# Sums of squares, decay sums and row broadcasts of a hybrid decoder trunk, put on TensorE in another form

## The chip, the cores and the metric

The kernel runs on one core of one Trainium2 chip, as one program in one launch. The metric is device time in microseconds (us); the engines are TensorE (PE, with its weight loads PEld), VectorE (DVE), ScalarE (ACT), GpSimd (POOL) and SyncE's DMA queue (SP).

## The reference

Two layers work on 512 tokens of width 1024. Each has a token-mixing part and a SwiGLU channel part of hidden width 2816, each behind an RMS norm with scale and shift from a conditioning vector. The mixing part projects the normed input once and feeds three causal mixers, whose outputs (512 + 256 + 256 columns) go through one output projection.

- A is a gated DeltaNet with four heads of width 128. Its queries and keys are normed per head, `x * rsqrt(sum(x*x) + 1e-6)`. With the gates g (16 numbers for each position of a 128-token block: 4 blocks and 4 heads) it needs the decay between any two positions, `exp(gcum[i] - gcum[j])` for i >= j, where gcum is the running sum of g.
- B is a chunked spatial-gating MLP.
- C is a sliding-window softmax attention with three patterns of window and dilation. The patterns' outputs are merged with weights that come from the softmax denominators: one number per token and head, times the 64 outputs of that head.

## The kernel before

Activations lie transposed: 128 channels in the partitions, 512 tokens along the free axis, so that a projection streams 512 columns. Exact float32 products are made of three one-pass matmuls: every weight tile and every activation tile is split into a rounded part `hi` (type fp32r, written by ScalarE) and the rest `lo` (VectorE), and `mm3` adds hi*hi, hi*lo and lo*hi. Small products stay in float32, which TensorE does in several passes; the trace shows them as two instructions.

The program is a set of tasks (Python generators). A planner (`Plan`, `Engine`) keeps a model of when each engine will be free, with costs per instruction, and at each step lets the task of best priority write its next instructions. The order of instructions on each engine is the order in which they were written; the engines work their queues in order. Priorities of the tasks stand in `PR0` and `PR1`, one set for each layer. Work tiles of 128x512 (`slot`) come from an arena of 58, PSUM banks (`bank`) from eight.

What the change touches:

- `loader` issues the weights' DMAs through four raw buffers; a transfer waits until the buffer four places before it is free. In the opening, each of eight chunks of the input needs two modulation reductions on VectorE, a scale on ScalarE, a product on VectorE, a rounded part on ScalarE and a low part on VectorE, and one weight tile; then 24 one-pass matmuls of the first projection use it. With the last of these weight tiles the loader also issues the DMA of the constant matrices (`cst`, among them the triangles `triu` and `slow`).
- `inv_rms` gives the norms' row scales: sums over channels by matmuls with one moving column, a reciprocal root on VectorE, and then a matmul for each block of 128 tokens that broadcasts the scales over the partitions. It is called for all four blocks in the opening and for half the tokens at a time in the six half norms after it.
- `sumsq_heads` gives the sums of squares of queries or keys. It is called for the keys (`kss`) and for the queries (`qss`) in both layers. ScalarE squares a head; a matmul with 32 columns of ones writes the sums to 32 partitions of one bank; after four heads ScalarE copies the bank, four transposes turn it, and VectorE reads 16 numbers per partition.
- `gates` makes g; `decay` multiplies the triangle `slow` by the g of each head (128x512 on VectorE), sums with `triu` in one float32 matmul of 512 columns, and takes the exponential. It runs four times in each layer.
- `merge` makes 16 merge weights per token on VectorE for each of two parts of C, and broadcasts them over the 64 rows of a head with 16 matmuls of 64 weight columns, eight in each bank. In each layer the out projection begins meanwhile and takes the merged tiles (`yc`) late in its order `Y_ORDER`.

Of the kernel before, what the change touches and what calls it, by code (L numbers as in the profile page):

```python
# [9 lines left out]
F32 = mybir.dt.float32  # L10
# [7 lines left out]
P = 128  # L18
# [265 lines left out]
def _trunk(ctx, tc, xT, cb, consts, prm, gmp, wmod, wt, wn, wab, wo, wo2, wf1, wf2, out):  # L284
# [24 lines left out]
    def slots(n, spare=0):  # L309

        yield arena.need(n + spare)
        return [slot() for _ in range(n)]

    def bank(n=1, spare=0):

        yield banks.need(n + spare)
        got = [banks.get() for _ in range(n)]
        return got[0] if n == 1 else got
# [11 lines left out]
    def b3(ap, n):  # L330
        return ap.rearrange("p (a b) -> p a b", a=n)
# [9 lines left out]
    def hs(h):  # L341
        return slice(h * P, (h + 1) * P)
# [15 lines left out]

    xs = [keep.tile([P, T], F32, name=f"xs{c}") for c in range(KC)]
    cst = keep.tile([P, C_N], F32, name="cst")  # L360
    cact = keep.tile([P, D], F32, name="cact")
    prs = [keep.tile([P, L_N], F32, name=f"pr{l}") for l in range(depth)]
    mods = [keep.tile([P, 48], F32, name=f"mod{l}") for l in range(depth)]
# [70 lines left out]
    def loader():  # L434
        def load_x():
            for c in range(KC):
                Q.dma_start(out=xs[c], in_=xT[:, c, :])
            Q.dma_start(out=cst[:, 0:C_TRIU], in_=consts[:, 0:C_TRIU])
            x_ok.done = True

        if X_AT < 0:
            load_x()
        for i, ((w, l, j), n, loose) in enumerate(pieces):
            yield lambda: 0.0 if len(raw_ok) < N_RAW or raw_ok[-N_RAW].done else None
            raw = ring("raw", n, F32, N_RAW)
            got = Flag()
            raw_ok.append(got)
            Q.dma_start(out=raw, in_=source[w][l, j])
            raws[w == "mod"].append((raw, got))
            if i == X_AT:  # L450
                load_x()
            if i == 3 * KC - 1:
                for l in range(1, depth):
                    Q.dma_start(out=prs[l], in_=prm[l])
                Q.dma_start(out=cst[:, C_TRIU:], in_=consts[:, C_TRIU:])
                cst_ok.done = True

    def modulation():
# [136 lines left out]
    def inv_rms(a, b0, n, warm=None):  # L595

        yield a[:, b0 * P:(b0 + n) * P]
        ps = yield from bank()
        for b in range(n):
            PE.matmul(ps[:, b:b + 1], a[:, hs(b0 + b)], ones[:, 0:1], start=True, stop=True)  # L600
        if warm:
            warm(a, 3)
        v = small(n)
        V.tensor_scalar(v, ps[:, 0:n], 1.0 / D, EPS, op0=ALU.mult, op1=ALU.add)
        bankf(ps)
        r = rsqrt(v, n)
        yield r
        rb = yield from bank()
        for b in range(n):
            PE.matmul(rb[:, hs(b0 + b)], r[:, b:b + 1].to_broadcast([P, P]), ident, start=True, stop=True)  # L610
        yield rb
        return rb

# [98 lines left out]
    def sumsq_heads(tiles):  # L712

        tiles = yield from all_of(tiles)
        ps = yield from bank()
        for h in range(NH):
            sq, = yield from slots(1)
            S.activation(sq, tiles[h], AF.Square)
            yield sq
            PE.matmul(ps[32 * h:32 * h + 32, :], ones[:, 0:32], sq, start=True, stop=True)  # L720
            free(sq)
        yield S, ps
        st, = yield from slots(1)
        S.activation(st, ps, AF.Copy)
        bankf(ps)
        yield st
        pt = yield from bank()
        for b in range(NB):
            PE.transpose(pt[:, hs(b)], st[:, hs(b)], ident)
        free(st)  # L730
        yield V, pt
        r = small(16)
        V.tensor_scalar(b3(r, NB), pt.rearrange("p (b h x) -> p b h x", b=NB, h=NH)[:, :, :, 0], EPS, None, op0=ALU.add)
        bankf(pt)
        return r

    def gates(ab, pr):

        xa, t, ea, g, beta = small(16), small(16), small(4), small(16), small(16)
        V.tensor_tensor(b3(xa, NB), ab[:, :, 0:4], every(pr[:, L_DTB:L_DTB + 4], NB, 4), op=ALU.add)  # L740
        V.tensor_scalar(t, xa, -1.0, None, op0=ALU.mult)
        V.tensor_tensor(t, xa, t, op=ALU.max)
        S.activation(ea, pr[:, L_ALOG:L_ALOG + 4], AF.Exp)
        S.activation(b3(beta, NB), ab[:, :, 4:8], AF.Tanh, scale=0.5)
        yield S, t
        S.activation(t, t, AF.Exp, scale=-1.0)
        S.activation(t, t, AF.Ln, bias=1.0)
        yield V, t
        V.scalar_tensor_tensor(t, xa, 0.0, t, op0=ALU.max, op1=ALU.add)
        V.scalar_tensor_tensor(b3(g, NB), b3(t, NB), -1.0, every(ea, NB, 4), op0=ALU.mult, op1=ALU.mult)  # L750
        V.tensor_scalar(beta, beta, 0.5, 0.5, op0=ALU.mult, op1=ALU.add)
        return g, beta

    def decay(c, g):

        gt, E = yield from slots(2, 4)
        V.tensor_tensor(b3(gt, NH), every(slow, NH, P), heads(g[:, 4 * c:4 * c + 4], NH, P), op=ALU.mult)
        yield gt
        ps = yield from bank()
        PE.matmul(ps, triu, gt, start=True, stop=True)  # L760
        free(gt)
        yield S, ps
        S.activation(E, ps, AF.Exp)
        bankf(ps)
        yield E
        G.tensor_tensor(b3(E, NH), b3(E, NH), every(tril, NH, P), op=ALU.mult)
        return E
# [493 lines left out]
    def merge(l, mls, atts, pairs, last):  # L1261


        oth = [small(32), small(32)]
        for i in (1 - last, last):
            yield atts[i]
            yield mls[i]
            Q.dma_start(out=mlscr[l][i], in_=mls[i].rearrange("p (b x) -> p b x", b=4))
            yield mlscr[l][i]
            for b in range(4):  # L1270
                if i == 0:
                    Q.dma_start(out=oth[1].rearrange("p (r x) -> p r x", r=4)[32 * b:32 * b + 32],
                                in_=mlscr[l][0].rearrange("(i r) b x -> b i r x", r=4)[b])
                else:
                    Q.dma_start(out=oth[0].rearrange("p (b x) -> p b x", b=4)[:, b, :],
                                in_=mlscr[l][1][32 * b:32 * b + 32].rearrange("i r x -> (i r) x"))
        oTs = [a.value for a in atts]
        for part in (last, 1 - last):
            yield V, oth[part]
            a = mls[part].rearrange("p (n s) -> p n s", s=2)  # L1280
            o = oth[part].rearrange("p (n s) -> p n s", s=2)
            m, ea, eo, t = small(16), small(16), small(16), small(16)
            V.tensor_tensor(m, a[:, :, 0], o[:, :, 0], op=ALU.min)
            V.tensor_tensor(ea, m, a[:, :, 0], op=ALU.subtract)
            V.tensor_tensor(eo, m, o[:, :, 0], op=ALU.subtract)
            yield S, ea, eo
            S.activation(ea, ea, AF.Exp)
            S.activation(eo, eo, AF.Exp)
            yield V, ea, eo
            V.tensor_tensor(eo, eo, o[:, :, 1], op=ALU.mult)  # L1290
            V.tensor_tensor(t, ea, a[:, :, 1], op=ALU.mult)
            V.tensor_tensor(t, t, eo, op=ALU.add)
            V.reciprocal(t, t)
            V.tensor_tensor(t, t, ea, op=ALU.mult)
            yield t
            for hp in range(2):
                ps = yield from bank()
                for b in range(4):
                    for e in range(2):
                        n = 4 * b + 2 * hp + e  # L1300
                        PE.matmul(ps[64 * e:64 * e + 64, hs(b)], t[:, n:n + 1].to_broadcast([P, 64]), ident,
                                  start=True, stop=True)
                yield V, ps
                V.tensor_tensor(oTs[part][hp], oTs[part][hp], ps, op=ALU.mult)
                bankf(ps)
        for hp in range(2):
            V.tensor_tensor(oTs[0][hp].rearrange("p (i r) -> p r i", r=4), oTs[0][hp].rearrange("p (i r) -> p r i", r=4),
                            oTs[1][hp].rearrange("p (r i) -> p r i", r=4), op=ALU.add)
            free(oTs[1][hp])
            yield S, oTs[0][hp]  # L1310
            split(oTs[0][hp], pairs[hp])
# [79 lines left out]
    def layer(l, h, kq):  # L1391
# [95 lines left out]
        def scales_of(gt, kss):  # L1487

            yield gt
            g, beta = gt.value  # L1490
            yield g
            ps = yield from bank()
            PE.matmul(ps[:, 0:16], triu, g, start=True, stop=True)
# [13 lines left out]

        def triangles(gt, kTs, scales):
            yield gt
            g = gt.value[0]  # L1510
            Es = [spawn(decay(c, g), rank()["E"], f"E{c}") for c in range(NB)]
            kT = yield from all_of(kTs)
            yield scales
# [293 lines left out]
```

## Time and profile before

| | us |
|---|---|
| median of 3 runs (lowest to highest) | 1484.37 (1483.23 to 1485.97) |
| the profiled execution | 1484.25 |
| its span, first to last instruction | 1482.5 |
| TensorE busy | 1460.3 |
| VectorE busy | 886.4 |
| ScalarE busy | 593.5 |
| GpSimd busy | 40.7 |

The span is the time from the first to the last recorded instruction; the execution's own time has 1.75 us more around it. All instructions are recorded by one helper, so every row carries the line L235 and is told apart by its tiles: `out<-moving,weights` for a matmul. There `cst` is a constant matrix, `w` a work tile, `s` a small tile, `hi` and `lo` the parts of a weight, `b` a bank. The mean granted clock of TensorE is 0.996 of full speed.

### The profile page before, as it was taken

Reading aid. Unit: us, or ns where it says so; the run is one execution under the profiler, and the core shown is the slowest. Engines: PE = TensorE matmul, PEld = TensorE weight load, DVE = VectorE, ACT = ScalarE, POOL = GpSimd, SP = SyncE. Lnnn points to the kernel's source line nnn. Section 1 sums busy time; section 2 is a strip of 40 time slices with the busy share of each in tenths; the row PEclk is TensorE's granted clock in tenths of the full one; section 3 lists DMA queues with packets and bytes.
Section 4 is the critical chain, followed back from the end, with each engine's and each line's share of the span. In section 5 each row is a group of like instructions: output and inputs, shape, how many; then the busy total and the mean of one; then the engine's idle time right before and its main releaser. Section 6 shows DMA issues by size and latency. Waiting matters only on the chain.

```text
span 1482.5 us, 19988 instructions
## 1 busy us (share of the span) xinstructions
PE 1460.3 (99%) x7810; PEld 1235.4 (83%) x7810; DVE 886.4 (60%) x1836; ACT 593.5 (40%) x1047; POOL 40.7 (3%) x60
## 2 busy tenths in 40 slices
PE   7999999999999999999999999999999999999998
PEld 5777998887988888888897889987789888888887
DVE  7788888946865555555476687656476333333332
ACT  4484426575432212222345533647544222222221
POOL 0001000000000000000000300100000000000000
PEclk9999999999999999999999999999999999999999
DMA  8723453503176665665322232121151332223331
GB/s 297 261 72 118 110 163 117 161 20 121 56 227 199 190 194 192 191 197 185 104 91 82 64 102 70 36 94 36 31 164 44 99 99 95 92 98 100 99 103 53
DMA packets 70638, 179.04 MB, mean 121 GB/s; under 512 B 25104, under 2 KB 25744, under 8 KB 70544
## 3 DMA queue, kind: packets, MB, share of 16 engines
q1 hardware_dynamic: 70544, 177.77, 37.5%
q8 instruction: 61, 1.00, 0.3%
q14 instruction: 33, 0.27, 0.1%
HBM read 174.53 MB, written 3.21 MB: 120 GB/s over the span
## 4 chain that ended last, share of the span: by engine, by line
PE 97%; DVE 1%; ACT 1%; DMA 0%; issue 0%; SPq 0%; ACTq 0%; DVEq 0%
PE b L235 97%; DVE w L235 1%; ACT w L235 1%; DMA xs<-in_xT_dram 0%; DVE s L235 0%; DVE raw L235 0%; DVE xs L235 0%; SPq L235 0%; DVE lo L235 0%; DVE mod L235 0%; ACT hi L235 0%; ACTq L235 0%; DVEq L235 0%
## 5 line engine op out<-in xcount | busy, mean ns | idle before, releaser
L235 PE MATMUL b<-w,hi 128*128 128x512 f32 (+1 forms) x2748 | 844.5, 389 | 2.5 <-ACT w L235 1.6
L235 PEld LDWEIGHTS b<-w,hi 128*128 128x128 f32 x2748 | 509.6, 188 | 110.8 <-issue 6.7
L235 PE MATMUL b<-w,lo 128*128 128x512 f32 (+1 forms) x1374 | 531.2, 387 | 0.0
L235 ACT ACTIVATE hi<-raw 128x1024 fp32r<-128x1024 f32 (+2 forms) x215 | 222.6, 1037 | 600.2 <-PE b L235 414.8
L235 DVE TENSOR_TENSOR lo<-raw,hi 128x1024 fp32r<-128x1024 f32 (+2 forms) x215 | 258.9, 1206 | 258.9 <-ACT hi L235 258.1
L235 PEld LDWEIGHTS b<-w,lo 128*128 128x128 f32 x1374 | 258.4, 188 | 52.3
L235 PE MATMUL b<-w,w 128*128 128x128 f32 (+2 forms) x1808 | 214.9, 284 | 4.0 <-ACT w L235 2.6
L235 PE MATMUL b<-hi,w 128*128 128x512 f32 (+2 forms) x768 | 214.8, 367 | 2.9 <-ACT w L235 2.9
L235 PEld LDWEIGHTS b<-w,w 128*128 128x128 f32 (+1 forms) x1808 | 199.2, 182 | 20.6 <-ACT w L235 10.2
L235 ACT ACTIVATE w<-b 128x512 f32<-128x512 f32 (+1 forms) x221 | 118.1, 560 | 137.0 <-PE b L235 126.0
L235 PEld LDWEIGHTS b<-hi,w 128*128 128x128 f32 x768 | 146.9, 213 | 24.1 <-issue 6.0
L235 PE MATMUL b<-lo,w 128*128 128x512 f32 (+2 forms) x384 | 137.7, 359 | 0.0
L235 DVE CUSTOM_DVE_ANT_0 raw<-raw,cact,pr 128x1024 f32<-128x1024 f32 x96 | 122.4, 1279 | 0.7 <-DMA raw<-in_wmod_dram 0.7
L235 DVE TENSOR_TENSOR w<-w,b 128x512 f32<-128x512 f32 x68 | 46.8, 688 | 125.5 <-PE b L235 124.7
L235 ACT ACTIVATE w<-w 128x512 f32<-128x512 f32 (+3 forms) x188 | 94.0, 519 | 22.9 <-DVE w L235 22.4
L235 PEld LDWEIGHTS b<-lo,w 128*128 128x128 f32 x384 | 81.4, 212 | 7.7
L235 DVE TENSOR_TENSOR w<-w,w 128x512 fp32r<-128x512 f32 (+2 forms) x104 | 68.1, 662 | 26.7 <-ACT w L235 26.1
L235 DVE SCALAR_TENSOR_TENSOR xs<-b,mod,xs 128x512 f32<-128x512 f32 (+1 forms) x56 | 37.1, 672 | 55.5 <-PE b L235 55.3
L235 PE MATMUL b<-cst,w 128*128 128x128 f32 (+1 forms) x416 | 57.5, 270 | 0.0
L235 PEld LDWEIGHTS b<-cst,w 128*128 128x128 f32 x416 | 49.4, 145 | 7.5 <-issue 1.0
L235 DVE SCALAR_TENSOR_TENSOR w<-w,cw,w 128x509 f32<-128x509 f32 (+2 forms) x72 | 51.8, 753 | 0.9 <-ACT w L235 0.2
L235 ACT ACTIVATE w<-w,mod 128x256 fp32r<-128x256 f32 (+1 forms) x56 | 29.8, 539 | 48.2 <-DVE w L235 48.2
(85 smaller groups left out, 652.4 us busy)
## 6 DMA issues: line engine op xcount, KB each, us to landing
raw<-in_wf_dram SPq DMA_DIRECT2D x132, 512.0 KB, 3.8
raw<-in_wmod_dram SPq DMA_DIRECT2D x96, 512.0 KB, 3.3
raw<-in_wt_dram SPq DMA_DIRECT2D x36, 512.0 KB, 3.5
raw<-in_wn_dram SPq DMA_DIRECT2D x36, 512.0 KB, 3.3
raw<-in_wo_dram SPq DMA_DIRECT2D x16, 320.0 KB, 2.9
raw<-in_wo_dram SPq DMA_DIRECT2D x6, 512.0 KB, 3.5
raw<-in_wab_dram SPq DMA_DIRECT2D x4, 544.0 KB, 5.7
xs<-in_xT_dram SPq DMA_DIRECT2D x8, 256.0 KB, 5.7
```

The lines of the kernel that those rows point to most:

```text
L235: r = f(*args, **kw)
```

## The change

`sumsq_heads` takes each square tile as weights, in blocks of 128 tokens, and streams one column of ones: 16 matmuls of one column in place of four of 512 columns, a ScalarE copy and four transposes. `gates` also splits g into a rounded part and the rest. `decay` makes one product tile for each part and sums both with a rounded copy of the triangle (`triur`) in two one-pass matmuls; it takes three slots where it took two. The copy `triur` is made once by ScalarE, right behind the issue of the constants' DMA. `inv_rms` broadcasts by a transpose of the broadcast column. `merge` writes the weights, broadcast over 64 columns, into two work tiles on VectorE and transposes these, four blocks in each bank. Neither the planner's costs nor the priorities are edited.

```diff
     cst = keep.tile([P, C_N], F32, name="cst")
+    triur = keep.tile([P, P], F32R, name="triur")
...
                 Q.dma_start(out=cst[:, C_TRIU:], in_=consts[:, C_TRIU:])
+                S.activation(triur, triu, AF.Copy)
...
         for b in range(n):
-            PE.matmul(rb[:, hs(b0 + b)], r[:, b:b + 1].to_broadcast([P, P]), ident, start=True, stop=True)
+            PE.transpose(rb[:, hs(b0 + b)], r[:, b:b + 1].to_broadcast([P, P]), ident)
...
             S.activation(sq, tiles[h], AF.Square)
             yield sq
-            PE.matmul(ps[32 * h:32 * h + 32, :], ones[:, 0:32], sq, start=True, stop=True)
+            for b in range(NB):
+                PE.matmul(ps[:, 4 * b + h:4 * b + h + 1], sq[:, hs(b)], ones[:, 0:1], start=True, stop=True)
             free(sq)
-        yield S, ps
-        st, = yield from slots(1)
-        S.activation(st, ps, AF.Copy)
+        yield V, ps
+        r = small(16)
+        V.tensor_scalar(r, ps[:, 0:16], EPS, None, op0=ALU.add)
         bankf(ps)
-        yield st
-        pt = yield from bank()
-        for b in range(NB):
-            PE.transpose(pt[:, hs(b)], st[:, hs(b)], ident)
...
-        return g, beta
+        gh, gl = small(16, F32R), small(16, F32R)
+        V.tensor_copy(gh, g)
+        V.tensor_tensor(gl, g, gh[:].bitcast(F32), op=ALU.subtract)
+        return g, beta, (gh, gl)
...
-        gt, E = yield from slots(2, 4)
-        V.tensor_tensor(b3(gt, NH), every(slow, NH, P), heads(g[:, 4 * c:4 * c + 4], NH, P), op=ALU.mult)
-        yield gt
+        yield arena.need(7)
+        gts = [slot(F32R) for _ in range(2)]
+        E = slot()
+        for gt, gp in zip(gts, g):
+            V.tensor_tensor(b3(gt, NH), every(slow, NH, P), heads(gp[:, 4 * c:4 * c + 4].bitcast(F32), NH, P), op=ALU.mult)
+        yield tuple(gts)
         ps = yield from bank()
-        PE.matmul(ps, triu, gt, start=True, stop=True)
-        free(gt)
+        PE.matmul(ps, triur, gts[0], start=True, stop=False)
+        PE.matmul(ps, triur, gts[1], start=False, stop=True)
+        free(*gts)
...
-            V.tensor_tensor(t, t, ea, op=ALU.mult)
-            yield t
+            tw = yield from slots(2)
+            four = lambda ap, hp: ap.rearrange("p (b i e o) -> p b i e o", b=4, i=2, o=1)[:, :, hp].to_broadcast([P, 4, 2, 64])
             for hp in range(2):
+                V.tensor_tensor(tw[hp].rearrange("p (b e j) -> p b e j", b=4, e=2), four(t, hp), four(ea, hp), op=ALU.mult)
+            for hp in range(2):
+                yield tw[hp]
                 ps = yield from bank()
                 for b in range(4):
-                    for e in range(2):
-                        n = 4 * b + 2 * hp + e
-                        PE.matmul(ps[64 * e:64 * e + 64, hs(b)], t[:, n:n + 1].to_broadcast([P, 64]), ident,
-                                  start=True, stop=True)
+                    PE.transpose(ps[:, hs(b)], tw[hp][:, hs(b)], ident)
+                free(tw[hp])
```

## Rows read from the trace of the kernel before

**Rows 1.** The page: busy us, share of the span and instructions of each engine.
```profile
PE 1460.3 (99%) x7810; PEld 1235.4 (83%) x7810; DVE 886.4 (60%) x1836; ACT 593.5 (40%) x1047; POOL 40.7 (3%) x60
```
**Rows 2.** The chain of waits in order of time: start us, us, what.
```profile
23.04 45.01 PE b L235 x190
...
73.43 155.73 PE b L235 x876
...
357.81 1.68 DVE w L235 x2
...
360.98 28.43 PE b L235 x196
```
**Rows 3.** Grouped matmuls, shapes kept apart: count, busy us, mean ns, idle before.
```profile
L235 PE MATMUL b<-w,cst 128*32 128x512 f32 x32 | 13.6, 605 | 0.0
...
L235 PE MATMUL b<-cst,s 128*64 128x128 f32 x128 | 7.9, 276 | 0.0
```
**Rows 4.** Timeline of TensorE from 83 to 90 us: start us, us, what.
```profile
85.50 1.05 PE L235 MATMUL b<-w,cst 128*32 128x512 f32 x2
...
87.03 1.05 PE L235 MATMUL b<-w,cst 128*32 128x512 f32 x4
...
88.48 0.41 PE L235 MATMUL b<-hi,w 128*128 128x264 f32 x2
...
88.84 0.41 PE L235 MATMUL b<-hi,w 128*128 128x264 f32 x2
...
89.21 0.60 PE L235 MATMUL b<-cst,w 128*128 128x128 f32 x4
89.57 0.49 PE L235 MATMUL b<-hi,w 128*128 128x264 f32 x2
```
**Rows 5.** Timeline of TensorE in two half norms, near 388 and 747 us.
```profile
388.08 0.60 PE L235 MATMUL b<-cst,s 128*128 128x128 f32 x4
388.44 0.96 PE L235 MATMUL b<-w,w 128*128 128x256 f32 x6
...
746.75 0.50 PE L235 MATMUL b<-cst,w 128*128 128x1 f32 x4
747.12 0.48 PE L235 MATMUL b<-w,hi 128*128 128x256 f32 x2
```
**Rows 6.** Timeline of TensorE from 113 to 119 us, the first layer's decays.
```profile
113.80 4.66 PE L235 MATMUL b<-w,cst 128*128 128x512 f32 x10
118.39 0.66 PE L235 MATMUL b<-cst,w 128*128 128x128 f32 x4
```
**Rows 7.** Timeline of TensorE from 348 to 352 us, around one merge.
```profile
348.82 0.62 PE L235 MATMUL b<-w,hi 128*128 128x512 f32 x2
349.28 0.39 PE L235 MATMUL b<-w,lo 128*128 128x512 f32 x1
349.59 1.97 PE L235 MATMUL b<-cst,s 128*64 128x128 f32 x32
351.49 0.73 PE L235 MATMUL b<-w,hi 128*128 128x512 f32 x2
```
**Rows 8.** Grouped instructions of VectorE, shapes kept apart.
```profile
L235 DVE SCALAR_TENSOR_TENSOR w<-xs,s,w 128x512 f32<-128x512 f32 x8 | 6.0, 746 | 0.0
...
L235 DVE TENSOR_TENSOR w<-cst,s 128x512 f32<-128x512 f32 x8 | 5.0, 687 | 0.0
```
**Rows 9.** Timeline of the DMA queue, first 100 us.
```profile
49.02 0.42 SPq L235 DMA_DIRECT2D cst<-in_consts_dram  x1
```
**Rows 10.** DMA issues: count, KB each, median us from issue to landing.
```profile
cst<-in_consts_dram SPq DMA_DIRECT2D x1, 712.0 KB, 6.7
```
**Rows 11.** Timeline of ScalarE from 47 to 60 us.
```profile
50.98 0.72 ACT L235 ACTIVATE w<-w,mod 128x512 fp32r<-128x512 f32 x1 [1.68 <-DVE w L235]
```
**Rows 12.** Stretches: us, TensorE busy (instructions), granted clock, DMA share, GB/s.
```profile
72.00:78.00 6.00, 5.60 (x24) 0.50 0.26 87
...
130.00:357.00 227.00, 226.16 (x1452) 1.00 0.38 116
```

More of the change, by code (lines that the diff above doesn't have):

```diff
@@ L719, in sumsq_heads @@
             yield sq
-            PE.matmul(ps[32 * h:32 * h + 32, :], ones[:, 0:32], sq, start=True, stop=True)
+            for b in range(NB):
+                PE.matmul(ps[:, 4 * b + h:4 * b + h + 1], sq[:, hs(b)], ones[:, 0:1], start=True, stop=True)
             free(sq)
-        yield S, ps
-        st, = yield from slots(1)
-        S.activation(st, ps, AF.Copy)
+        yield V, ps
+        r = small(16)
+        V.tensor_scalar(r, ps[:, 0:16], EPS, None, op0=ALU.add)
         bankf(ps)
-        yield st
-        pt = yield from bank()
-        for b in range(NB):
-            PE.transpose(pt[:, hs(b)], st[:, hs(b)], ident)
[L730 to L734, printed above, removed]
         return r
@@ L1489, in scales_of @@
             yield gt
-            g, beta = gt.value
+            g, beta, _ = gt.value
             yield g
@@ L1509, in triangles @@
             yield gt
-            g = gt.value[0]
+            g = gt.value[2]
             Es = [spawn(decay(c, g), rank()["E"], f"E{c}") for c in range(NB)]
```

## The prediction

> **What bounds the kernel now.** I read the page first: TensorE is busy 99% of the span, VectorE 60%, ScalarE 40% [rows 1]. Then the chain of waits in order of time: it is long stretches of TensorE work, with short breaks in which another engine is named. The two stretches that matter here run from 23.04 (the first projection, 45.01 us) and from 73.43 (155.73 us); the wait at 357.81 is the end of the first layer's merge [rows 2]. So an instruction taken off TensorE inside a stretch is worth what it occupies there, and work added to VectorE or ScalarE costs nothing as long as TensorE has other work. TensorE's time isn't read from the durations, which overlap, but from the distance between starts in the timeline. The grouped rows give the counts: a float32 matmul stands as two instructions (16 matmuls of the sums of squares as x32, 64 of the merge as x128) [rows 3], a transpose as one.
>
> **1. Squares as weights** (four calls: keys and queries, two layers). Removed in each: four matmuls of the ones against 512 columns and four transposes. In the timeline one such matmul starts at 85.50 and the next one at 87.03, with one ordinary triple of 264 columns between; an undisturbed triple takes 88.84 - 88.48 = 0.36. So a matmul occupies 1.53 - 0.36 = 1.17 us [rows 4]. The row at 87.03 holds four instructions in no more time (87.03 to 88.48, a triple included): two matmuls into different column groups ran side by side [rows 4]. The 32 instructions [rows 3] stand in 13 such slots, one of them inside a train without edges (0.92, below): 12 x 1.17 + 0.92 = 15.0. Four transposes take 89.57 - 89.21 = 0.36 [rows 4], with the slower first load after them some 0.45, four times: 1.8. Together 16.8 us.
> Added: 64 matmuls with the squares as 128x128 weights and one moving column. The first norm has that form: two of them (four instructions) start at 746.75 and the next work at 747.12, 0.37 us [rows 5]. A group of four is then 0.74 and, with about 0.09 of edge as for the transposes, 0.83; sixteen groups, since each square comes on its own: 13.3 us. Gain 3.5 us. Bounds: without edges 11.8 (gain 5.0); at 0.9 per group with an edge on both sides 14.4 (gain 2.4). I take 3.5, because the 0.37 is of the same form at full clock.
> The Trainium skill ("TensorE: Matmul & The Clock Gate", section "LDWEIGHTS") says that a weight load costs its number of columns at 1.2 GHz whatever streams past; that estimate is 107 ns a load, 13.7 us for 128 loads and a gain of 3.1. The trace has 92 ns an instruction [rows 5] and decides.
> A copy on ScalarE and a round trip over TensorE also go, but the scales that wait for them have a stretch of other matmuls in front of them. I count nothing; without that cover it would be a gain of about a microsecond a layer.
>
> **2. Decay sums.** Eight float32 matmuls of 512 columns become sixteen one-pass ones. Before, ten such instructions (four decays and one matmul of part 1) run from 113.80 to 118.39: 0.46 each, 0.92 a decay [rows 6]. A one-pass 512-column matmul of the projections occupies 0.23 (the pair from 348.82 to 349.28) [rows 7]; two are 0.46. Gain 8 x 0.46 = 3.7 us. Bounds: 3.0, if a load between different weights shows each time, to 3.7. VectorE gets a second 0.687 us product for each decay [rows 8] and two small operations in the gates. The first layer's decays fall in the stretch from 73.43, in which TensorE has its own work, so I count nothing. If it ran dry there, 4 x 0.69 = 2.8 us in a layer would show. The third slot that a decay asks for can hold it back; the trace doesn't show how many are free.
>
> **3. Row scales of the norms.** Two broadcast matmuls are four instructions from 388.08 to 388.44 [rows 5]: 90 ns each. Transposes are one instruction of 90 ns [rows 4], so a half norm saves 0.18; six halves: 1.1 us. The four of the opening lie in a stretch where TensorE isn't the bound: nothing. Bounds 0.9 to 1.5.
>
> **4. Merge.** Four times 16 matmuls of 64 weight columns, 32 instructions, from 349.59 to 351.49: 1.90; the single matmul at 349.28 takes 0.31 until they start, where 0.23 is usual [rows 7], and as much is lost after them by estimate: 2.1. After: eight transposes at 0.09, in two groups with an edge of 0.09 each: 0.9. Per merge 1.2, together 4.8 us of TensorE. But the scales' product grows from a 16-column one to two of 512 columns (0.69 each, VectorE), and in the first layer the chain of waits runs through the merge: TensorE's matmul at 360.98 waits for what VectorE began at 357.81 [rows 2]. What TensorE saves there in front of that wait, 2.4 us, comes back only as far as the chain shortens too. It loses 1.9 of matmuls and gains 1.2 of products and 0.4 of transposes in series: about 0.3 shorter, more if the queue order improves. I take 1.1 of the 2.4 for the first layer and all 2.4 of the second, where no such wait stands: 3.5 us. Bounds 2.4 to 4.8.
>
> **5. The rounded triangle.** A copy of 128x128 goes to ScalarE's queue right behind the DMA that brings the triangle. That DMA (712 KB) is issued at 49.02 and takes 6.7 us to land [rows 9, 10]: 55.7. ScalarE works in order. The loader gets there as soon as the second reduction of the seventh of eight chunks is written into the program, while that chunk's scale and rounded input wait for the reduction's planned end; so they stand behind the copy in ScalarE's order. The rounded input, made at 50.98 before [rows 11], then comes at about 55.7 + 0.3 for the copy + 0.4 for the scale (both estimates) + 0.75 for the product on VectorE [rows 8] + 0.72 [rows 11] = 57.9, its low part 0.75 later. TensorE wants it when six of eight chunks of the 45.01 us are done, at 23.04 + 33.8 = 56.8 [rows 2]. It waits about 1.1 for the first and some 0.5 more for the low part: a loss of 1.5 us. From below, 0: the landing is the last packet's, and the planner can put the copy behind that chunk. From above 2.6 (the rounding of one weight tile, some 1.1, also ahead of that input), and 3 more if the clock falls after it: the stretch from 72 to 78, behind a gap of the same kind, ran at 0.50 [rows 12], 1.2 GHz, so half of its 6 us was lost.
>
> **Sum.** -3.5 - 3.7 - 1.1 - 3.5 + 1.5 = -10.3 us. The profiled execution took 1484.25 us (span 1482.5, 1.75 outside it); the median of the runs is 1484.37, the same within 0.01%. Forecast 1474.0.
>
> **Rivals.**
> *More than counted.* No stall at the copy, groups without edges, the whole merge: -5.0 - 3.7 - 1.5 - 4.8 = -15.0, 1469.3. For it: all four prices are of forms that stand in the trace; against it: the copy's place in the queue.
> *Eaten by waits.* The order of the whole program is written anew by a planner that counts these costs, with priorities left as they are. If parts 1 and 4 give their lower bounds (2.4 each), part 2 gives 3.0, part 3 0.9, and the copy costs its upper 5.6: -3.1, 1481.2. For it: the present order leaves TensorE 1% idle, so it has more to lose than to win; against it: a wait must appear on TensorE, which had work almost everywhere.
> *The clock falls (slower).* The squares' groups have one column where 512 streamed. If each of the four calls, and the wait of part 5, is followed by a stretch like that from 72 to 78, five times 3 us are lost: 1474 + 15 = 1489. It decides from four such stretches on (1474 + 12 = 1486). For it: that stretch shows that thin work brings the clock to 0.50. Against it: from 130 to 357, with most of the transposes inside, it stayed at 1.00 [rows 12].
> The Trainium skill (same page, section "Part 4: PE-mode transpose") says that transposes don't count as busy for the clock, which speaks against parts 3 and 4; the row from 130 to 357 doesn't show a fall, though matmuls lie between.
> *Nothing gained.* Transposes by another way that cost what the matmuls did: parts 3 and 4 fall away and 1, 2 and 5 leave -5.7, 1478.6. I see no row for it, since transposes stand at 90 ns.
>
> **How the numbers follow.** Chances: forecast 0.55 (own range 1470.5 to 1477.5), more than counted 0.13, eaten by waits 0.20, clock 0.08, nothing gained on the broadcasts 0.04. A change under 0.2% (3 us) is about what the measurement can't tell from none. Faster by that means under 1481.4: the forecast, more than counted, the broadcasts' rival and half of eaten: 0.82, less 0.02 for stacked mishaps: 0.80. Same, the other half and a third of the clock's: 0.13. Slower, the rest: 0.07. The range leaves out half of the clock's case and the ends of the outer ones: 1468.5 to 1482.0.
>
> **What would show it.** Right: TensorE's busy time about 1450; 128 instructions of one column in sixteen groups, 0.8 us from start to next work; no 128x32 and 128x64 weights of these names; decays 0.46 apart per pair; the copy of the triangle on ScalarE at about 55.7 and a TensorE gap of 1 to 2 us near 57. Wrong: granted clock below 1.00 behind the squares; a new wait of several microseconds in a mixing stage, above all for a decay or a merge product; a one-column matmul at clearly over 0.2 us.

## The result and the profile after

The change made the kernel slower: 1499.11 us (median of 6 runs, 1497.67 to 1504.35) beside 1484.70 for before, ratio 1.0106 [1.0086, 1.0126]. The forecast was 1474.0, its range ended at 1482.0, and slower had a chance of 0.07. The profiled execution took 1503.73 us with a span of 1502.0: it is the second longest of the six and has their lowest granted clock, 0.983, where the others have 0.986 to 0.990, so its loss to the clock is above that of a median execution (by some 5 us, an estimate from its distance to the median).

The page of the changed kernel answers to [rows 1] (busy us, share of the span, instructions):

```profile
PE 1466.6 (98%) x7778; PEld 1255.0 (84%) x7778; DVE 900.0 (60%) x1852; ACT 589.6 (39%) x1043; POOL 45.3 (3%) x60
```

TensorE has 32 instructions fewer and is busy 6.3 us longer. To read that, split its time in three. Idle is span less busy: 22.2 us before, 35.4 after. Lost to the clock is busy time times (1 - granted clock), summed over all stretches of 2 us: 4.9 before, 23.3 after. What is left is its work at full clock: 1455.4 before, 1443.3 after. So **12.1 us of work went**, much what the prices of parts 1 to 4 said, and 13.2 us of idle time and, in this execution, 18.4 us of slow clock came in.

Grouped matmuls of the changed kernel, shapes apart, answer to [rows 3] (count, busy us, mean ns, idle before). The 128x32 and 128x64 weights of the two removed groups are gone; 128 of the 160 one-column instructions are the squares, the rest the first norm's.

```profile
L235 PE MATMUL b<-cst,w 128*128 128x1 f32 x160 | 22.0, 263 | 3.2 <-ACT w L235 3.2
...
L235 PE MATMUL b<-w,triur 128*128 128x512 f32 x16 | 5.0, 395 | 0.0
```

The timeline of TensorE behind the first squares, the answer to [rows 4], and the stretch that follows (us, busy, granted clock, DMA share, GB/s):

```profile
87.33 3.63 PE L235 MATMUL b<-cst,w 128*128 128x1 f32 x32
90.82 0.49 PE L235 MATMUL b<-hi,w 128*128 128x264 f32 x2
...
92.02 0.65 PE L235 MATMUL b<-hi,w 128*128 128x264 f32 x2
```

```profile
92.00:94.00 2.00, 2.00 (x11) 0.50 0.00 0
...
818.00:820.00 2.00, 0.87 (x9) 0.76 0.52 201
...
826.00:828.00 2.00, 2.00 (x11) 0.50 0.00 0
```

Sixteen matmuls take 3.49 us, 0.87 a group of four. TensorE never waits in them, yet from 92.0 it is granted 0.50 of its clock, 1.2 GHz, and a pair of 264 columns that takes 0.40 us takes 0.65. Around the squares of the second layer, which have one wait of 1.13 us among them, it lasts from 819 to 829. About 10 of the 23.3 us lost lie around one-column groups (92 to 96, 112 to 120, 819 to 829); the others follow waits, in the opening, near 76, 350, 776 and 1104 us.

Where the idle time is, the chain of waits shows (start us, us, what). Before, it was TensorE alone from 73.43 for 155.73 us [rows 2]:

```profile
77.15 13.82 PE b L235 x98
91.17 3.97 DVE w L235 x6
95.82 1.28 ACT L235
97.11 1.21 ACT w L235 x4
...
110.59 1.25 ACT w L235 x2
111.88 233.38 PE b L235 x1444
```

For 21 us, from 91.17 to 111.88, the end is set by VectorE and ScalarE; TensorE's one-column groups at 103.41, 109.18 and 111.88 wait 0.70, 0.50 and 0.85 us there. The second place is the merge of the second layer (the wait stands in brackets):

```profile
1099.20 1.03 PE L235 MATMUL b<-cst,w 128*128 128x128 f32 x8
1102.84 0.79 PE L235 MATMUL b<-w,hi 128*128 128x512 f32 x1 [2.61 <-ACT w L235]
1104.72 0.79 PE L235 MATMUL b<-w,hi 128*128 128x512 f32 x1 [1.08 <-DVE w L235]
```

The eight transposes have nothing behind them. What they release (VectorE's products at 1099.84 and sum at 1101.04, ScalarE's rounding at 1102.16) runs in series while TensorE stands still, and the clock is 0.57 over the 8 us from 1102. By TensorE's waits, compared with those of before, the added idle time is some 3.7 us here, 2.7 around the first layer's merge, 2.1 in the stretch from 91 to 112, 2.2 in the opening, 1.1 in the second layer's squares and 0.8 near 61.

### The profile page after: what moved, and what is told of

It reads as the page before. It is cut to its first block, busy times and chain, and to the rows that moved or that the text cites. A ratio compares the mean times of both kernels' runs of the same rounds, so it can differ in the third digit from the quotient of the medians.

```text
span 1502.0 us, 19949 instructions
## 1 busy us (share of the span) xinstructions
PE 1466.6 (98%) x7778; PEld 1255.0 (84%) x7778; DVE 900.0 (60%) x1852; ACT 589.6 (39%) x1043; POOL 45.3 (3%) x60
## 4 chain that ended last, share of the span: by engine, by line
PE 93%; DVE 3%; ACT 2%; DMA 1%; issue 1%; SPq 0%; DVEq 0%; ACTq 0%
PE b L235 93%; DVE w L235 2%; ACT w L235 1%; DVE s L235 0%; DVE lo L235 0%; DMA cst<-in_consts_dram 0%; ACT hi L235 0%; DMA xs<-in_xT_dram 0%; ACT L235 0%; DVE raw L235 0%; DMA raw<-in_wt_dram 0%; SPq L235 0%; DVE xs L235 0%; ACT s L235 0%; DVEq L235 0%
## 5 line engine op out<-in xcount | busy, mean ns | idle before, releaser
L235 PE MATMUL b<-w,w 128*128 128x128 f32 (+2 forms) x1808 | 220.9, 287 | 5.1 <-ACT w L235 3.8
L235 PEld LDWEIGHTS b<-w,w 128*128 128x128 f32 (+1 forms) x1808 | 203.8, 185 | 22.7 <-ACT w L235 12.3
L235 PE MATMUL b<-cst,w 128*128 128x128 f32 (+1 forms) x560 | 78.3, 272 | 3.2 <-ACT w L235 3.2
L235 PEld LDWEIGHTS b<-cst,w 128*128 128x128 f32 x560 | 69.1, 162 | 11.7 <-ACT w L235 5.0
```

Of the source, the lines that this page charges most:

```text
L235: r = f(*args, **kw)
```

## The experiments

The planner writes the order of every engine's queue from prices. With runs of equal instructions taken as one line and the two traces compared line by line, at least 107 of the 3722 lines of TensorE's queue in before, 63 of ScalarE's 725 and 174 of VectorE's 1523 are gone or stand elsewhere in the changed kernel; with the change's instructions in the place of the old ones (the last runs below) it is 23, 5 and 6. These counts are from below, since the traces leave buffer numbers out; the expectations count otherwise and give larger ones. The runs therefore separate **order** from **instructions**: a kernel "in the order of before" carries a recorded list of the planner's turns. Each run has the ratio to before, run beside it on the same chip, with a 95% interval.

### Order against instructions, first attempt

The changed kernel let go in the recorded turns of before, and before in those of the changed kernel:

```
+TURNS = (recorded list of task names, one for each turn)
+Plan.run = run_in_turns        # takes the next recorded task in place of the best priority
```

> The changed kernel's instructions, written in the order of turns that the tasks took in the kernel before, so that each queue differs only where an instruction was replaced. Theory A (the new order of the queues costs the time, the new instructions save what the prediction counted): 1473 to 1479 us. Theory B (the new instructions themselves lower the clock, wherever they stand): 1493 to 1502 us, with granted clock 0.50 behind the one-column groups.

1512.69 us, 1.0190 [1.0175, 1.0205]: worse than the changed kernel in its own order.

> The converse: the instructions of the kernel before in the order of turns of the changed kernel. Theory A: 1500 to 1512 us, as slow as the changed kernel or slower by the saving. Theory B: 1482 to 1488 us.

1503.47 us, 1.0132 [1.0115, 1.0149]: not one instruction of the change is in it. Its work at full clock is 1452.4 (1463.5 busy, 11.1 lost to the clock), its idle time 39.3. Its chain of waits begins the same stretch with the pieces that the changed kernel has; here they last from 88.39 to 100.80, and after 6.00 us of TensorE VectorE and ScalarE set the end for 6.9 more:

```profile
88.57 3.97 DVE w L235 x6
...
93.21 1.28 ACT L235
...
100.80 6.00 PE b L235 x16
```

So the order alone can cost all of it, and yet undoing the order made things worse: neither theory holds as it was put. In the first run the changed parts take other numbers of turns than the old ones, so it was not the old order after all; the run of the change in the same place, below, mends that.

### Is it a wrong price in the planner?

```
-            full = 0.0004167 * (256 if passes == 4 and n <= 64 and m == 128 else n) * passes * ...
+            full = 0.0004167 * (112 if passes == 4 and n <= 64 and m == 128 else n) * passes * ...
```

> The changed kernel; only the planner's price of a float32 matmul with a short moving operand goes from 0.43 to 0.19 us, which is what the rows show. Theory A with the wrong price as its cause: 1474 to 1482 us. Theory A with the cause elsewhere (any new order is worse than the one that the priorities were chosen for): 1488 to 1502 us. Theory B: 1497 to 1502 us.

1501.58 us, 1.0119 [1.0098, 1.0140]. Putting the planner's price of a short float32 matmul right, from 0.43 us to the 0.2 or so of the trace, gained nothing: that price by itself isn't the cause, but a new price makes a new order too, so this is not a test of the price alone.

### The parts alone

The merge by transposes alone. It was planned anew, though its expectation says that the order stays; by the traces 4 lines of TensorE's queue, 2 of ScalarE's and 9 of VectorE's are gone or stand elsewhere:

> Only the merge is changed; the order of every queue stays as before except for the replaced instructions. By the prediction's part 4: 3.5 us less (2.4 to 4.8), 1480 to 1482.5 us. Theory B (transposes lower the clock): 1484 us or more. If the first layer's wait for the merge eats it: 1484 us.

1488.13 us, 1.0028 [1.0019, 1.0038]. TensorE's timeline at the end of the second layer's mixing part has the changed kernel's two waits:

```profile
1084.15 1.06 PE L235 MATMUL b<-cst,w 128*128 128x128 f32 x8
1087.77 0.51 PE L235 MATMUL b<-w,hi 128*128 128x512 f32 x1 [2.56 <-ACT w L235]
1089.63 0.79 PE L235 MATMUL b<-w,hi 128*128 128x512 f32 x1 [1.36 <-DVE w L235]
```

Squares alone, in the turns of before:

> Part 1 alone (squares as weights), in the order of turns of the kernel before. By the prediction's price: 3.5 us less, 1480 us, clock 1.00 around the groups. By the clock's rival: behind the groups of both layers the granted clock falls to 0.50 for some 3.4 us each, 1.7 us lost every time; with three or four such stretches 1482 to 1488 us.

1487.29 us, 1.0024 [1.0015, 1.0034]. TensorE's work at full clock is 3.3 us less than before, close to the counted 3.5, and the clock takes 5.0 more. Behind the squares (timeline, then stretches):

```profile
84.00 0.95 PE L235 MATMUL b<-cst,w 128*128 128x1 f32 x8
84.81 0.49 PE L235 MATMUL b<-hi,w 128*128 128x264 f32 x2
...
85.26 1.84 PE L235 MATMUL b<-cst,w 128*128 128x1 f32 x16
86.96 0.49 PE L235 MATMUL b<-hi,w 128*128 128x264 f32 x2
```

```profile
88.00:90.00 2.00, 2.00 (x11) 0.50 0.00 0
```

Decay sums with the triangle copy, in the turns of before, and the same with the copy moved to the first decay:

```
-                S.activation(triur, triu, AF.Copy)          # behind the DMA
...
+        if not tri_ok.done:                                 # in decay()
+            S.activation(triur, triu, AF.Copy)
+            tri_ok.done = True
```

> Part 2 with part 5 alone (decay sums by parts of g, triangle copied right behind its DMA), in the order of turns of the kernel before. By the prediction: -3.7 + 1.5, 1481 to 1482 us. If the copy holds ScalarE up as in the first run, where TensorE lost 6.3 us between 56 and 68: 1484 to 1488 us.

1487.55 us, 1.0021 [1.0011, 1.0032]. TensorE stands as forecast behind ScalarE's copy, and longer: 2.31 and 0.61 us, with the clock at 0.54 from 60 to 62. The copy, and TensorE's two waits:

```profile
55.45 0.31 ACT L235 ACTIVATE triur<-cst 128x128 fp32r<-128x128 f32 x1 [9.23 <-DMA cst<-in_consts_dram]
```

```profile
59.44 0.50 PE L235 MATMUL b<-w,hi 128*128 128x512 f32 x1 [2.31 <-ACT w L235]
60.55 0.79 PE L235 MATMUL b<-w,hi 128*128 128x512 f32 x1 [0.61 <-DVE w L235]
```

> As the run before, but the copy of the triangle is written at the first decay instead of behind the DMA. If the copy's place is what costs: 1478 to 1481 us, 4 to 6 us under the run before, and no TensorE gap near 57. If the copy is free: as the run before.

1482.30 us, 0.9987 [0.9978, 0.9996]: the gap is gone, and the copy's place is worth 5.2 us.

The norm rows alone, in the turns of before, then planned anew:

> Part 3 alone (row scales by transposes), in the order of turns of the kernel before: by the prediction 1.1 us less, 1482.5 us; if transposes let the clock fall at the norm's waits (760 to 766), 1484 to 1487 us.

1483.70 us, 1.0005 [0.9995, 1.0014].

> The norm part alone, but planned anew: almost the same instructions as before (the norm part alone in the old order measured 1.0005 of before), while 416 lines of TensorE's queue stand elsewhere. If any order that the planner writes anew loses against the order before (theory A as it stands after the first runs: the old order is a lucky one), 1490 to 1503 us with 6 to 15 us more of idle TensorE. If orders of the planner are as good as each other and only the orders with the merge's transposes lose, 1481 to 1486.

1492.86 us, 1.0066 [1.0051, 1.0082]. The same instructions in another order (at least 64 of the 3722 lines of TensorE's queue moved) cost 9 us: 30.4 us idle for 22.2, with the clock loss as before (4.7).

### One column or the form

Squares as weights in the turns of before, with 128 columns of ones streamed where one was. Here each head has a bank of its own, and VectorE reads the sums head by head:

```
-                PE.matmul(ps[:, 4 * b + h:4 * b + h + 1], sq[:, hs(b)], ones[:, 0:1], start=True, stop=True)
+                PE.matmul(ps[:, hs(b)], sq[:, hs(b)], ones, start=True, stop=True)
```

> Squares as weights as in the change, but with 128 moving columns of ones in place of one column: the same number of instructions and of weight loads, each four some 0.83 to 0.95 us as before; the rest of the old order. If it is the one-column stream that makes the clock fall behind these groups, the clock stays at 1.00 at 86 to 92, 808 to 812 and 834 to 842 us and the time is 1479.5 to 1482.5. If it is the weight loads or the form itself, the half-clock stretches stay and it is 1486 to 1489.

1483.59 us, 0.9998 [0.9990, 1.0007]. As many instructions, as many weights, 0.85 us a group as with one column, and the clock stays:

```profile
83.58 1.95 PE L235 MATMUL b<-cst,w 128*128 128x128 f32 x16
85.29 0.49 PE L235 MATMUL b<-hi,w 128*128 128x264 f32 x2
```

```profile
88.00:90.00 2.00, 2.00 (x12) 1.00 0.00 0
```

So it is the one-column stream, and not the weights or the form, behind which the clock falls; since banks and turns differ a little between these two runs, the pair in the changed kernel's order (below) tells it more cleanly. The time falls between the two expectations: the clock came back, but the work saved did not come out as time.

### Place: a handful of lines

Two attempts kept the old turns but not the old place. The first has transposes for the first merge part only; the second all parts, each mended (128 columns, late copy, that merge):

```
+            if part == last:
+                ... the two products and the transposes of the change
+            else:
+                ... the matmuls of before
```

> The merge by transposes for the first of its two parts only; the last part keeps the matmuls against the unit vectors, in the old order. If the layer-1 end waits (2.56 and 1.36 us, with the half clock behind them) are what made the merge alone 1.0028 of before, they go, and the time is 1481.5 to 1484. If transposes cost by themselves (clock), 1487 to 1489 again.

1500.96 us, 1.0118 [1.0104, 1.0132].

> All parts in the order of turns of before: squares as weights with 128 moving columns, the decay sums in two matmuls with the triangle copy written at the first decay, the norm rows by transposes, the merge by transposes for its first part only. If the parts add up and the losses were the three places named (clock behind one column, copy behind the DMA, transposes at the layer's end), 1475 to 1480. If parts hinder each other through the ring buffers whatever they are, 1486 to 1505.

1505.77 us, 1.0145 [1.0131, 1.0159]. Both missed. In the first only some 6 lines of TensorE's queue, 4 of ScalarE's and 12 of VectorE's stand otherwise than in before, and TensorE waits 4.34 us at the merge of each layer, and 1.8 ahead of it; that is 12.3 of the 13.7 us of added idle time. In the first layer:

```profile
365.30 0.50 PE L235 MATMUL b<-w,hi 128*128 128x512 f32 x1 [4.34 <-ACT w L235]
```

ScalarE and VectorE at the same time:

```profile
360.81 0.74 ACT L235 ACTIVATE hi<-raw 128x640 fp32r<-128x640 f32 x1 [8.32 <-issue]
...
364.62 0.63 ACT L235 ACTIVATE w<-w 128x512 fp32r<-128x512 f32 x1 [2.03 <-DVE w L235]
```

```profile
361.59 0.83 DVE L235 TENSOR_TENSOR lo<-raw,hi 128x640 fp32r<-128x640 f32 x1 [5.60 <-ACT hi L235]
...
362.93 0.68 DVE L235 TENSOR_TENSOR w<-w,b 128x512 f32<-128x512 f32 x1
363.53 1.06 DVE L235 TENSOR_TENSOR w<-w,w 128x512 f32<-128x512 f32 x1
```

The merge's product (362.93) stands in VectorE's queue behind the `lo` split of a weight, which waits for the `hi` split on ScalarE, which starts only at 360.81, when TensorE has begun its last matmuls in front of the wait (360.57 and before). That its buffer came free there is read from the times and not tried. TensorE then waits for the product: a ring of queues.

So the merge was written with as many turns as the old one (the two products at the turn of the old product of t, no turn between), which leaves all three engines' queues as in before but for its own instructions:

```
-                yield tw[hp]
                 ps = yield from bank()
```

> The merge by transposes in both parts, and every other instruction of TensorE, VectorE and ScalarE exactly where before has it: the transposes stand where the matmuls stood, with the same output-projection matmuls behind them, and the two products where the small product of t stood. If the waits of the merge alone (2.56 and 1.36 us at the end of layer 1, ratio 1.0028) came from where the queue put the transposes, they are gone and the time is that of before less what the merge's matmuls give back (four times 1.97 less 1.03): 1479.5 to 1482. If the longer chain (two products of 0.65 us for one of 0.17) is the cause wherever it stands, 1485 to 1490.

1483.34 us, 0.9999 [0.9990, 1.0007]. The waits of 2.56 and 1.36 are gone. Work fell by 4.2 us (1451.2), yet the time stayed: the two 0.65 us products are late for the second pair of transposes, in both layers.

```profile
355.60 1.23 PE L235 MATMUL b<-cst,w 128*128 128x128 f32 x8 [1.52 <-DVE w L235]
...
1084.51 1.23 PE L235 MATMUL b<-cst,w 128*128 128x128 f32 x8 [1.52 <-DVE w L235]
```

Then three parts, and all parts, in place. So that the squares keep their turns too, each head's matmuls overwrite all but the columns already wanted, and turns without work stand for those that the change leaves out:

```
+                PE.matmul(ps[:, P * b + h:P * b + P], sq[:, hs(b)], ones[:, h:P], start=True, stop=True)
```

> Squares as weights (125 to 128 columns), the decay sums in two matmuls with the triangle copy at the first decay, the norm rows by transposes; no change of the merge; everything else where before has it. If the parts add up once each instruction stays in its place and the clock is kept, the counted 3.5, 3.7 and 1.1 us come out at least by half: 1475 to 1480. If TensorE's savings are eaten by the engines that feed it whatever the order, 1481 to 1485.

1481.29 us, 0.9982 [0.9973, 0.9991], the best of all: faster than both kernels.

> The same with the merge by transposes in both parts in the place of its matmuls: the whole change with the clock kept, the triangle copy late and the old order. If place and clock were the whole loss, 1471 to 1478, the forecast's own range. If parts hinder each other through the ring buffers, 1484 to 1505 as in the first attempt at all parts.

1483.02 us, 0.9990 [0.9982, 0.9999]. Work fell by 11.6 us (1443.8, as in the changed kernel), the span by 0.4; idle time rose by 8.2 and the clock loss by 3.0. Of the 8.2 us, 3.9 are three new waits before the merges' transposes (1.53, 0.85 and 1.53) and 2.5 two that came with the three parts. One of these, on TensorE, in the run of the three parts:

```profile
136.28 1.16 PE L235 MATMUL b<-w 128*128 128x128 f32 x8 [1.54 <-DVE w L235]
```

TensorE comes to these transposes 1.5 us before VectorE has their input; before, it had no wait there.

### The table of two by two

The last runs: the changed kernel in its own order with 125 to 128 columns for one; the change as it is with every other instruction in the place of before; and the mended parts planned anew.

> The changed kernel in its own order, instruction for instruction, but each weight of squares streams 125 to 128 columns of ones in place of one. If the one-column streams cost the changed kernel the clock, most of the stretches near 92, 108 to 120 and 818 to 830 us stand at 1.00 and the time is 1487 to 1494; the order's idle time of some 35 us stays. If the clock falls there for another cause, 1497 to 1501.

1502.55 us, 1.0125 [1.0112, 1.0139]: no better than the changed kernel. The falls at 92 and from 819 to 829 are gone, with the order the same instruction for instruction, 32 instructions in 3.49 us as there, and a wait of 1.02 us among the second layer's squares for 1.13 there:

```profile
92.00:94.00 2.00, 2.00 (x15) 1.00 0.00 0
...
820.00:822.00 2.00, 1.52 (x13) 1.00 0.00 0
```

This is the cleanest pair for the cause of these falls; what lies between one and 125 columns wasn't tried. Yet the time did not follow. Against the profiled execution of the changed kernel the clock gave back 10.3 us (13.0 lost for 23.3), idle time took 5.8 of it, and 3.1 us more work stood against it; against that kernel's other executions, at a granted clock of 0.986 to 0.990 for the 0.990 here, hardly any clock came back, for new falls stand at 104 and 126 us behind new waits. The chain of waits still runs over ScalarE and VectorE where the clock was low, two of its pieces and the next long one of TensorE:

```profile
100.68 1.28 ACT L235
...
117.26 8.09 DVE w L235 x8
125.40 221.75 PE b L235 x1377
```

> The change as it is (one column of ones, the triangle copy right behind the constants' DMA, both merge parts by transposes), but every instruction that it doesn't touch where before has it. With one edit each for the clock and for the copy undone in the same order the time was 1483.0; squares with one column alone lost 1.0024 to the clock and the early copy cost some 5 us against the late one. If order and these two add up, 1490 to 1496, so that of the changed kernel's loss about half is the order. If the order is nearly all of it, 1484 to 1488; if it is none of it, 1498 to 1504.

1494.50 us, 1.0069 [1.0056, 1.0082]. The rows of its stretches: the copy's gap, then the squares of both layers:

```profile
56.00:66.00 10.00, 6.74 (x22) 0.83 0.59 198
90.00:100.00 10.00, 10.00 (x49) 0.66 0.10 31
814.00:824.00 10.00, 10.00 (x59) 0.66 0.01 2
846.00:850.00 4.00, 4.00 (x24) 0.57 0.00 0
```

From the rows, 3.3 us are idle at the copy and 10 us go to the clock: 6.74 x 0.17 + 10 x 0.34 + 10 x 0.34 + 4 x 0.43 = 9.7. Mended, the same order is 1494.50 - 1483.02 = 11.5 us faster.

> The counterpart: all parts with 128 columns and the late copy, as in the run that gave 1483.0 in the old order, but in an order that the planner makes anew (some 650 lines of TensorE's queue differ from before). If the new order costs by itself what the old instructions lost in it (19 us) and the norm rows planned anew (9 us), 1492 to 1503. If the mends are enough, 1481 to 1487.

1488.20 us, 1.0033 [1.0022, 1.0044].

| | order of before, to the instruction | an order planned anew |
|---|---|---|
| the change as it is | 1.0069 | 1.0106 |
| 128 columns, late copy | 0.9990 | 1.0033 |

Down the left column 0.79% (some 11 us) are the one-column clock and the early copy, with the order kept. Across a row 0.37% and 0.43% (some 6 us) are the order. Down the right column the orders differ as well, since these two kernels are planned separately, so its 0.73% isn't shown to be those two alone: in the changed kernel's own order 128 columns gave nothing back. Nor do the costs add up: old instructions in the changed kernel's order lost 1.3%.

## Why the prediction was wrong, point by point

**The step that failed.** The sum took what each part frees on TensorE as time, and put two terms at nothing: the new order of all queues, and the clock behind the squares. The work did go (12.1 us). But old instructions in the changed kernel's order alone took some 20 us more than before (1.0132), the squares alone cost 5.0 us more clock, and even with order, clock and copy mended 11.6 us less work gave 0.4 us of span.

**What bounds the kernel.** "Work added to VectorE or ScalarE costs nothing as long as TensorE has other work" was right as a sentence, and the reading that it has such work almost everywhere failed. TensorE was 99% busy while several of the chains that feed it arrived just in time: with all parts in place, 11.6 us of saved work brought 8.2 us of new idle time. An instruction off TensorE was therefore not worth what it occupied.

**Part 1.** The price held: 0.81 for a group alone and 0.85 to 0.87 for groups in a row, for 0.83; work down 3.3 us for 3.5. At 106 to 109 ns an instruction in a row, the slower of the two rates that were weighed fits better than the 92 that I took. What failed is the weight of the clock's rival, 0.08. Its form was right (a fall behind the squares, to 0.50): squares alone lost 5.0 us more to the clock than before. I had called the row from 130 to 357 at 1.00 [rows 12] evidence against it, but that row has nothing of one column in it. The row that I read as thin work, 72 to 78 at 0.50, stands behind waits of TensorE, the first of them

```profile
69.70 0.51 PE L235 MATMUL b<-hi,w 128*128 128x264 f32 x2 [1.45 <-ACT w L235]
```

and two more of 0.61 us, so it spoke of a fall behind idle time. The pairs of runs with one and with 128 columns tell the two apart. A price of the four one-column instructions of the first norm [rows 5] says nothing of what 16 or 32 in a row do to the clock.

The Trainium skill ("TensorE: Matmul & The Clock Gate", section "LDWEIGHTS") gives a weight load its columns at 1.2 GHz; the estimate of 107 ns agrees with these 106 to 109, and was nearer than the row that I let decide.

**Part 2.** Right: 0.46 a decay, as the timeline of the changed kernel has it (answer to [rows 6]); with the copy late, work fell by 3.1 us, for 3.7 with a lower bound of 3.0.

```profile
121.25 0.63 PE L235 MATMUL b<-w,triur 128*128 128x512 f32 x2
121.71 0.62 PE L235 MATMUL b<-w,hi 128*128 128x512 f32 x2
```

**Part 3.** Counted 1.1; work down 1.8, time unchanged within the measurement.

**Part 4.** What failed is "all 2.4 of the second, where no such wait stands". In the kernel before, the second layer's merge is as tight as the first's. In both a pair of matmuls that takes 0.62 elsewhere is stretched, because its second half is released by VectorE only 0.04 us before it starts; from the start of the first half to that of the second 0.44 and 0.37 us pass where 0.23 is usual:

```profile
360.54 0.94 PE L235 MATMUL b<-w,hi 128*128 128x512 f32 x2
...
1087.52 0.88 PE L235 MATMUL b<-w,hi 128*128 128x512 f32 x2
```

The chain of waits names only the first. In the changed kernel the second layer's merge waits 2.61 and 1.08, in the old place 1.52. The transposes save TensorE 4.2 us; the two products on VectorE take them back. Alone, the merge is worth nothing in the old place and costs 0.28% as the planner orders it; added to the three other parts in place it cost 1.7 us.

**Part 5.** The mechanism was right and the size depends on the order: 5.2 us in the order of before, for the 1.5 taken and the upper bound of 5.6. In the changed kernel itself the copy runs at 57.13 and TensorE waits 0.77, with no fall of the clock behind it:

```profile
57.13 0.31 ACT L235 ACTIVATE triur<-cst 128x128 fp32r<-128x128 f32 x1 [9.82 <-DMA cst<-in_consts_dram]
```

**The rivals.** "Eaten by waits" named the cause (the order is written anew, 1% idle has more to lose than to win) and then priced it from the parts' lower bounds, 1481.2, still a gain. It had no term for an order that loses. The runs give that term: 9 us for the norm rows, some 20 for the old instructions in the changed kernel's order. Two mechanisms thus came together, each on the slow side, where I had let each stand alone. Of the signs named for wrong, two came: the clock below 1.00 behind the squares, and a wait of 2.61 us for a merge. "Nothing gained" on the broadcasts is excluded: the merge's transposes took 4.2 us off TensorE.

**Open.** Which decision of the planner costs the 21 us stretch from 91 to 112 wasn't tried; putting the price of short matmuls right didn't help. And in the changed kernel's own order the clock's share can't be told apart: the falls behind the squares went without a gain in time, while in the order of before the two mends together gave 11.5 us.

## What to carry to other kernels

When a planner or a scheduler writes the queues, a change of prices changes every queue: keep the old order to the instruction while a change is judged, and put a spread for a new order (here 6 to 20 us of 1484) into the forecast. That an engine is 99% busy says that its feeders arrive in time, not that they have slack; look how late each chain arrives at the place where the saving lands. Where data become weights and one column is left to stream, look at the granted clock behind it before counting the gain: here 128 columns cost no more time than one and left the clock at 1.00.

## What the hardware showed that was not expected

Sixteen weights of 128x128 with one moving column took 3.49 us in a row and were followed by a granted clock of 0.50; with 125 to 128 moving columns in the same order they take the same 3.49 us and the clock stays at 1.00. And a few moved instructions weigh more than many removed ones: the change in the turns of before (1.0190) and in the exact place of before (1.0069) differ by some 18 us, with some 5 lines of TensorE's queue, 4 of ScalarE's and 17 of VectorE's standing otherwise.
